# The DRAM sums of an encoder's weights: an earlier start, a wider spacing, and one issuing engine

## The chip, the cores and the metric

The kernel runs on one core of a Trainium2 chip. The metric is the device time in microseconds of one execution, the median over the runs of one kernel; fewer is better. A profile is one execution taken by the hardware profiler, with its own time.

The engines in the profile are PE (TensorE; PEld is its weight load), DVE (VectorE), ACT (ScalarE), POOL (GpSimd) and SP (SyncE, which here only issues transfers). ACT, POOL and SP each issue DMA transfers from their own instruction queue, in the order of that queue.

## What is computed

Two layers of an encoder on 256 positions of 2048 channels, in float32. Each layer has a mixer and a gated feed-forward part, with a norm ahead of each and a residual sum behind it. Cut to what matters here:

```python
for layer in range(2):
    h = rms_norm(x, norm_mix[layer])
    if layer % 2 == 0:
        ...                                  # pooling and grouped-query attention, one output projection
    else:
        mixed = mlstm_mixer(h, ...)          # matrix memory in 8 heads, gates, one output projection
    x = x + mixed
    x = x + conv_ffn(rms_norm(x, norm_ffn[layer]), w_up[layer], conv_w[layer], conv_b[layer], w_down[layer])

def conv_ffn(x, w_up, conv_w, conv_b, w_down):
    u = x @ w_up                             # 2048 -> 2 x 5632
    u = conv of width 3 over the positions of u, plus conv_b
    gate, val = jnp.split(u, 2, axis=-1)
    return (jax.nn.silu(gate) * val) @ w_down   # 5632 -> 2048
```

## The kernel before

**Weights.** All weights stream through SBUF in pieces of 128 x 1024 float32 (512 KB). `Stream.load` (line 107) issues one transfer on SP's queue, up to five pieces ahead. `Stream.split` makes a high part on ACT (line 127) and a low part, the rest, on DVE (line 128), up to two pieces ahead; these are the tiles `hl`. Every product is three matmuls (high by high, high by low, low by high), all recorded at line 256. There are six `wraw` buffers for loaded pieces and four `wsplit` buffers for split ones.

**Feed-forward layers.** The 44 pairs of up tiles are done in chunks of 4, 8, 8, 8, 8 and 8 (`FCH`). An up tile (`up`) takes four pieces and 64 matmuls, then the convolution and the gate. Between the up tiles of a chunk stand the down products of the chunk before. For some halves of the output columns these are done by a scheme that needs seven products of blocks in place of eight (`unit`, matmuls into `pp`); it needs sums of weight blocks. `_halves` says for which: half 1 in every chunk but the last, half 0 as well in the chunks 2 to 4 of layer 0 and 1 to 4 of layer 1. `unit` of half 1 runs in the first four slots of the next chunk, that of half 0 in the last four.

**Sums of weight blocks.** For half 1 they are made on the fly: `Stream.prepare` loads a piece on SP (line 112, tile `sum`, three buffers) and adds another to it by an accumulating transfer on GpSimd's queue (line 113); the further sums of that pair are made on DVE in `split` (lines 123 and 124, a `Chain`). For half 0 they are made ahead of time in DRAM by `premix`: 12 in layer 0 and 16 in layer 1, one for each pair of rows of blocks. Each takes five transfers: two copies into the scratch tile `m` (here on ACT's queue), one accumulate of a third block, and two accumulates of half a piece from `m` into `m`, all three on GpSimd's queue. `Stream.load` then reads `m` as it reads any weight (`w<-m`).

**What sets the order.** PE's instructions stand in program order. The other engines' are put in order by a scheduler when the program is built, with waits put in where data asks for them. A `Weave` holds a clock of its own: every part of a product ticks it by an estimate of its matmuls' time, and generators that were added with a delay get on when it has passed. `premix(layer, gap, late)` adds one generator a sum with `aside`: the first eight start `gap` apart and the others `late` apart, in units of that clock (about a microsecond); the steps of one lie 0.2, 1.2, 1.2 and 1.2 gaps apart. `paced` makes each of these transfers wait for the matmul that was issued last at that place of the program. The end of the last step hands the tile to `Stream.load`.

**Norms.** `Norm.finish` takes the inverse square root with a `pow` on GpSimd (line 263) between two steps of DVE. For norms 0 and 2 it sends the result through DRAM and back by two transfers on GpSimd's queue (`rr` line 340, `R` line 342). `scaled` in the mLSTM layer reads `R` (line 821).

Of the kernel before, what the change touches and what calls it, by code (L numbers as in the profile page):

```python
# [32 lines left out]
FCH = [4, 8, 8, 8, 8, 8]  # L33
# [174 lines left out]
def trunk(ctx: ExitStack, tc: tile.TileContext, gx, xT, xn, call, catt, cml, weights, mixes, out):  # L208
    nc = tc.nc
    v, a, g, pe = nc.vector, nc.scalar, nc.gpsimd, nc.tensor  # L210
# [241 lines left out]
    def paced(ins):  # L452

        tc.add_manual_dep(ins.ins, last_mm[0].ins.name, now, reason="paced")

    def premix(layer, gap, late):

        def one(i, s0, s1, r, made):
            m = scratch.tile([P, 2, CH * P], F32, tag=f"m{layer}{i}", name=f"m{layer}_{i}")
            h = CH * P // 2  # L460
            steps = [(nc.scalar, m[:, 0], s0, {}, 0.2), (nc.scalar, m[:, 1], r, {}, 1.2),
                     (g, m[:, 0], s1, add, 1.2), (g, m[:, 1, :h], m[:, 0, :h], add, 1.2),
                     (g, m[:, 1, h:], m[:, 1, :h], add, 0.0)]
            for eng, to, src, kw, wait in steps:
                paced(eng.dma_start(to, src, **kw))
                if wait:
                    yield wait * gap
            for j in range(2):
                made[j].ap = m[:, j]

        for i, e in enumerate(mixes[layer]):
            wv.aside(one(i, *e), min(i + 1, 8) * gap + max(i - 7, 0) * late)
# [275 lines left out]
    def mlstm_layer(norm, nxt):  # L748
        with ExitStack() as es:
# [171 lines left out]

            hns, done = {}, set()
            wv.add(norm.finish(), 6.0)
            premix(1, 28.0, 28.0)
            for hp in range(MH // 2):
                vf = t1p.tile([P, 2, 512], F32, tag="vf", name=f"mvf{hp}")
                for c, n in ((0, MD + 32), (MD, MD)) if hp == 0 else ((0, 512),):
# [26 lines left out]
    def ffn_layer(layer, norm, nxt):  # L954
        with ExitStack() as es:
# [16 lines left out]
            def up(c, f, gt, i):  # L972
                ps = stat_group(xx, list(range(KT)), f"up{layer}_{f}")
                wv.until(lambda: norm.R is not None)
                u = gather(tp, ps, f"up{layer}_{f}")
                v.tensor_mul(u, u, bc(norm.R, 2))  # L976
                y = tp.tile([P, 2, S], F32, tag="y", name=f"y{layer}_{f}")
                z = t1p.tile([P, 2, 2, S], F32, tag="z", name=f"z{layer}_{f}")
                for j in range(2):
                    tl = f + j * FT  # L980
                    a.activation(z[:, 0, j, :], u[:, j, :], AF.Copy, scale=cw(tl, 0))  # L981
                    a.activation(z[:, 1, j, :], u[:, j, :], AF.Copy, scale=cw(tl, 2))
                    a.activation(y[:, j, :], u[:, j, :], AF.Identity, scale=cw(tl, 1), bias=cw(tl, 3))  # L983
                v.tensor_add(y[:, :, 1:S], y[:, :, 1:S], z[:, 0, :, 0 : S - 1])  # L984
                v.tensor_add(y[:, :, 0 : S - 1], y[:, :, 0 : S - 1], z[:, 1, :, 1:S])
                if i % 2 == 0:
                    quads[c, i // 2] = tp.tile([P, 4, P], F32, tag="silu", bufs=3, name=f"s{layer}_{f}")
                s_ = quads[c, i // 2][:, i % 2 * 2 : i % 2 * 2 + 2].rearrange("p a b -> p (a b)")
                a.activation(s_, y[:, 0, :], AF.Silu)
                v.tensor_mul(s_, s_, y[:, 1, :])  # L990
                a.copy(gt[:, i, 0, :], s_)
                v.tensor_sub(gt[:, i, 1, :], s_, gt[:, i, 0, :].bitcast(F32))

            def combine(c, j):

                g4 = quads.pop((c, j))
                sf = sm1.tile([P, 512], F32, tag="sq", name=f"sf{layer}_{c}_{j}").rearrange("p (a b) -> p a b", a=4)
                v.tensor_sub(sf[:, 0:2], g4[:, 0::3], g4[:, 1:2].to_broadcast([P, 2, P]))
                v.tensor_add(sf[:, 2], sf[:, 1], g4[:, 0])
                v.tensor_sub(sf[:, 3], sf[:, 2], g4[:, 2])  # L1000
                s3 = kp.tile([P, 2, 3, P], F32R, tag=f"s3{j}", name=f"s3{layer}_{c}_{j}")
                s1 = st.sums.tile([P, 2, P], F32R, tag=f"s1{j}", name=f"s1{layer}_{c}_{j}")
                for d, e in ((s3, sf[:, 0:3]), (s1, sf[:, 3])):
                    a.copy(d[:, 0], e)
                    v.tensor_sub(d[:, 1], e, d[:, 0].bitcast(F32))
                combos[c, j] = s3, s1
# [104 lines left out]
            def down(c, b):  # L1111
                gt, last = gts[c], c == len(FCH) - 1
                kts = list(range(FCH[c]))
                if last and nxt is None and b == NB - 1:
                    down_end(gt, b, kts)
                    return
                ps = mmp.tile([P, 2, 512], F32, tag="mm", name=f"dn{layer}_{c}_{b}")
                mov_part(ps, lambda k: gt[:, k], kts, True, True)
                if last:
                    wv.until(lambda: ("total", 1) in pss)  # L1120
                residual(ps, b)
                if last and nxt is None:
                    nc.sync.dma_start(out[:, :, b * 512 : b * 512 + 512], x[:, :, b * 512 : b * 512 + 512])
                elif last:
                    nxt.add(b)

            def down_two(c):

                gt, n = gts[c], FCH[c]
                pss2 = [mmp.tile([P, 2, 512], F32, tag="mm", name=f"dn{layer}_{c}_{b}") for b in range(2)]  # L1130
                for kts in (range(n - 2), range(n - 2, n)):
                    for ps in pss2:
                        mov_part(ps, lambda k: gt[:, k], list(kts), kts[0] == 0, kts[-1] == n - 1)
                wv.until(lambda: 0 not in seen or ("total", 0) in pss)
                for b, ps in enumerate(pss2):
                    residual(ps, b)
                    if nxt is None:
                        nc.sync.dma_start(out[:, :, b * 512 : b * 512 + 512], x[:, :, b * 512 : b * 512 + 512])
                    else:
                        nxt.add(b)  # L1140
# [3 lines left out]
            for kind, c, i, *j in _ffn_plan(layer):  # L1144
                if kind == "up":
                    if i == 0:
                        gts.append(actp.tile([P, 8, 2, S], F32R, tag=f"B{c % 2}", name=f"g{layer}_{c}"))
                    up(c, f, gts[c], i)
                    f += 1
                elif kind == "down":  # L1150
                    down(c, i)
                elif kind == "two":
                    down_two(c)
                elif kind == "mix":
                    combine(c, i)
                else:
                    unit(kind, c, i, *j)
# [3 lines left out]
    attention_layer(norms[0], norms[1])  # L1161
    norms.append(Norm(2))
    ffn_layer(0, norms[1], norms[2])
    norms.append(Norm(3))
    mlstm_layer(norms[2], norms[3])
    ffn_layer(1, norms[3], None)


# [55 lines left out]
def _ffn_plan(layer):  # L1224

    seq = []  # L1230
    for c, n in enumerate(FCH):
        pairs = FCH[c - 1] // 2 if c else 0
        halves = _halves(layer, c - 1)

        if halves == (0, 1):
            slots = [[(kind, c - 1, h, js)] for h in (1, 0) for kind in "AB" for js in ((0, 1), (2, 3))]
        else:
            slots = [[(kind, c - 1, 1, (j,))] for kind in "AB" for j in range(pairs)]
            for b in range(2 if pairs else 0):
                slots[(b + 1) * pairs // 2 - 1].append(("down", c - 1, b))  # L1240

        busy = {j: k for k, slot in enumerate(slots) for u in slot if u[0] == "A" for j in u[3]}
        for i in range(n):
            seq.append(("up", c, i))
            seq += slots[i] if i < len(slots) else []
            if c < len(FCH) - 1:
                seq += [("mix", c, j) for j in range(n // 2) if i == max(2 * j + 1, busy.get(j, 0))]
    return seq + [("two", len(FCH) - 1, 0)] + [("down", len(FCH) - 1, b) for b in range(2, NB)]
# [156 lines left out]
```

## Time and profile before

| | |
|---|---|
| median of 3 runs | 2174.39 us (2172.65 to 2174.52) |
| profiled execution | 2172.38 us |
| its span, from the first to the last instruction | 2170.4 us |
| granted TensorE clock | 1.00 |
| HBM read and written over the span | 539.50 and 60.86 MB, 277 GB/s |
| stages by the span | attention layer to 260, feed-forward layer 0 to 972, mLSTM layer to 1453, feed-forward layer 1 to the end |

A busy row gives time, share of the span and number of instructions. In a row of a group, the part after the bar is the busy time and the mean of one, and after the next bar the engine's idle time just before them and what ended most of it. A name with a small q behind the engine (ACTq, POOLq, SPq) is the queue's part: it issues a transfer and the engine itself stays idle. GpSimd's own issues stand as POOL and count as busy. An arrow after an idle time points to what ended the wait. A row of transfers gives the queue that issued them, their number, the size of one and the median time from issue to landing.

### The profile page before, as it was taken

To read this page: it belongs to the slowest core of one execution; us is meant where nothing else is said; L and a number is where in the kernel's file an instruction comes from. 1 tells how busy PE (TensorE), PEld (TensorE's weight loads), DVE (VectorE), ACT (ScalarE), POOL (GpSimd) and SP (SyncE) were. 2 spreads that over 40 slices of the span, in tenths; PEclk is the share of its full clock that TensorE was granted. 3 is DMA by queue.
4 is the path that set the end of the run, shared out by engine and by line. 5 is a ranking of instruction groups with operands and counts; after the bars stand their busy time and mean duration, and the time that the engine had idled before them with its cause. 6 is when DMAs were issued, how large, how long until landed. Compare 5 with 4: busy or idle time off the path is not lost.

```text
span 2170.4 us, 31559 instructions
## 1 busy us (share of the span) xinstructions
PE 2160.9 (100%) x11424; PEld 1845.4 (85%) x11424; DVE 1729.7 (80%) x2428; ACT 1406.7 (65%) x2200; POOL 128.7 (6%) x160
## 2 busy tenths in 40 slices
PE   9999999999999999999999999999999999999999
PEld 7888888888888888889888888888888888888887
DVE  7686678887988888976777676667888898988896
ACT  7665576766677767666554554457676777776763
POOL 0011010000000000000000010110000000000000
PEclk9999999999999999999999999999999999999999
DMA  9668988787988877757688888998978787887774
GB/s 326 220 204 255 287 247 263 231 268 243 293 272 278 281 247 234 253 193 226 203 250 248 252 243 243 276 274 249 270 214 283 253 272 248 264 266 242 233 252 163
DMA packets 157790, 543.72 MB, mean 251 GB/s; under 512 B 17498, under 2 KB 19842, under 8 KB 157634
## 3 DMA queue, kind: packets, MB, share of 16 engines
q1 hardware_dynamic: 129056, 460.10, 61.1%
q0 software_dynamic: 17440, 48.51, 13.5%
q10 hardware_dynamic: 11138, 33.11, 4.6%
q8 instruction: 89, 1.46, 0.3%
q14 instruction: 67, 0.55, 0.1%
HBM read 539.50 MB, written 60.86 MB: 277 GB/s over the span
## 4 chain that ended last, share of the span: by engine, by line
PE 92%; DVE 4%; DMA 3%; issue 1%; ACT 1%; DVEq 0%; ACTq 0%; POOLq 0%
PE up L256 40%; PE pp L256 11%; PE op L256 8%; PE dn L256 6%; PE mv L256 4%; PE mq L256 4%; PE mk L256 4%; PE mo L256 4%; PE qproj L256 3%; DVE hl L128 2%; DMA w<-in_dn 1%; PE kproj L256 1%; PE vproj L256 1%; DMA sum<-in_dn 1%; PE pool L256 1%
## 5 line engine op out<-in xcount | busy, mean ns | idle before, releaser
L128 DVE TENSOR_TENSOR hl<-w,hl 128x1024 fp32r<-128x1024 f32 (+2 forms) x836 | 1002.8, 1211 | 223.3 <-ACT hl L127 220.6
L127 ACT CAST hl<-w 128x1024 fp32r<-128x1024 f32 (+2 forms) x835 | 857.2, 1043 | 450.5 <-PE up L256 134.3
L256 PE MATMUL up<-xx,hl 128*128 128x512 f32 (+1 forms) x5632 | 996.6, 337 | 3.2 <-DVE hl L128 3.0
L256 PEld LDWEIGHTS up<-xx,hl 128*128 128x128 f32 x5632 | 865.9, 188 | 137.9 <-DVE hl L128 7.9
L256 PE MATMUL pp<-hl,s 128*128 128x512 f32 x768 | 193.2, 393 | 0.4 <-DVE hl L128 0.4
L256 PEld LDWEIGHTS pp<-hl,s 128*128 128x128 f32 x768 | 141.3, 188 | 30.2 <-DVE hl L128 1.6
L256 PE MATMUL pp<-hl,g 128*128 128x512 f32 x576 | 147.9, 391 | 0.0
L419 ACT COPY tb_up<-up 128x512 f32<-128x512 f32 x88 | 51.6, 586 | 113.0 <-PE up L256 112.8
L256 PEld LDWEIGHTS pp<-hl,g 128*128 128x128 f32 x576 | 105.4, 188 | 20.7
L256 PE MATMUL dn<-hl,g 128*128 128x512 f32 x528 | 122.7, 390 | 0.0
L256 PEld LDWEIGHTS dn<-hl,g 128*128 128x128 f32 x528 | 98.7, 188 | 20.3
L983 ACT ACTIVATE y<-tb_up,cst 128x256 f32<-128x256 f32 x176 | 103.6, 589 | 0.0
L984 DVE TENSOR_TENSOR y<-y,z 128x510 f32<-128x510 f32 x88 | 60.5, 688 | 50.2 <-ACT y L983 50.2
L981 ACT ACTIVATE z<-tb_up,cst 128x256 f32<-128x256 f32 x176 | 88.4, 502 | 7.9 <-DVE tb_up L976 6.4
L256 PE MATMUL mk<-xx,hl 128*128 128x512 f32 (+1 forms) x512 | 92.1, 337 | 0.0
L256 PE MATMUL mq<-xx,hl 128*128 128x512 f32 (+1 forms) x512 | 92.1, 337 | 0.0
L256 PE MATMUL mv<-hl,xx 128*128 128x512 f32 (+2 forms) x480 | 91.7, 350 | 0.0
L256 PE MATMUL op<-hl,cat 128*128 128x512 f32 x384 | 91.6, 393 | 0.0
L420 DVE TENSOR_TENSOR tb_up<-up,tb_up 128x512 f32<-128x512 f32 x88 | 60.6, 688 | 38.4 <-ACT tb_up L419 38.4
L256 PE MATMUL mo<-hl,xx 128*128 128x512 f32 x384 | 90.5, 391 | 0.0
L256 PE MATMUL op<-hl,mcat 128*128 128x512 f32 x384 | 89.5, 392 | 0.0
L256 PEld LDWEIGHTS mq<-xx,hl 128*128 128x128 f32 x512 | 79.2, 188 | 11.6
(232 smaller groups left out, 2097.0 us busy)
## 6 DMA issues: line engine op xcount, KB each, us to landing
w<-in_up SPq DMA_DIRECT2D x352, 512.0 KB, 4.8
w<-in_dn SPq DMA_DIRECT2D x176, 512.0 KB, 4.5
w<-in_m_in SPq DMA_DIRECT2D x124, 512.0 KB, 5.3
m<-in_dn ACTq DMA_DIRECT2D x56, 512.0 KB, 6.0
w<-m SPq DMA_DIRECT2D x56, 512.0 KB, 4.8
w<-in_a_in SPq DMA_DIRECT2D x46, 512.0 KB, 4.8
sum<-in_dn SPq DMA_DIRECT2D x36, 512.0 KB, 4.9
sum<-in_dn POOLq DMA_DIRECT2D x36, 512.0 KB, 8.9
```

Of the source, the lines that this page charges most:

```text
L127: (self.nc.vector.tensor_copy if i + c == 0 else self.nc.scalar.copy)(hl[:, 0, c : c + n], w[:, c : c + n])
L128: self.nc.vector.tensor_sub(hl[:, 1, c : c + n], w[:, c : c + n], hl[:, 0, c : c + n].bitcast(F32))
L256: last_mm[0] = pe.matmul(out_, lhsT, rhs, start=start, stop=stop, skip_group_check=True)
L419: a.copy(tb, ps[:, :, 1, :])
L420: v.tensor_add(tb, ps[:, :, 0, :], tb)
L981: a.activation(z[:, 0, j, :], u[:, j, :], AF.Copy, scale=cw(tl, 0))
L983: a.activation(y[:, j, :], u[:, j, :], AF.Identity, scale=cw(tl, 1), bias=cw(tl, 3))
L984: v.tensor_add(y[:, :, 1:S], y[:, :, 1:S], z[:, 0, :, 0 : S - 1])
```

## The change

All five transfers of each sum are issued by GpSimd, in both layers. `premix` for layer 1 is called in feed-forward layer 0, in its last chunk after the up tile i = 4, and no longer at the start of the mLSTM layer; its gaps are 46 units and no longer 28. Those of layer 0 stay at 26 and 90.

```diff
         def one(i, s0, s1, r, made):
             m = scratch.tile([P, 2, CH * P], F32, tag=f"m{layer}{i}", name=f"m{layer}_{i}")
             h = CH * P // 2
-            steps = [(nc.scalar, m[:, 0], s0, {}, 0.2), (nc.scalar, m[:, 1], r, {}, 1.2),
+            steps = [(g, m[:, 0], s0, {}, 0.2), (g, m[:, 1], r, {}, 1.2),
                      (g, m[:, 0], s1, add, 1.2), (g, m[:, 1, :h], m[:, 0, :h], add, 1.2),
                      (g, m[:, 1, h:], m[:, 1, :h], add, 0.0)]
...
             wv.add(norm.finish(), 6.0)
-            premix(1, 28.0, 28.0)
             for hp in range(MH // 2):
...
                     up(c, f, gts[c], i)
                     f += 1
+                    if layer == 0 and c == len(FCH) - 1 and i == 4:
+                        premix(1, 46.0, 46.0)
                 elif kind == "down":
```

## Prediction

> **What bounds the kernel now.** I read the page first (busy time, chain that ended last, costliest groups), then a table of busy time by stage, then the rows of the moved transfers.
>
> ```profile
> PE 2160.9 (100%) x11424; PEld 1845.4 (85%) x11424; DVE 1729.7 (80%) x2428; ACT 1406.7 (65%) x2200; POOL 128.7 (6%) x160
> ...
> PE 92%; DVE 4%; DMA 3%; issue 1%; ACT 1%; DVEq 0%; ACTq 0%; POOLq 0%
> ...
> L256 PE MATMUL up<-xx,hl 128*128 128x512 f32 (+1 forms) x5632 | 996.6, 337 | 3.2 <-DVE hl L128 3.0
> ```
>
> TensorE (PE) is busy for 2160.9 of 2170.4 us; the other rows hang on it. What a change of transfers can win is bounded by PE's idle time, so I ask where that lies. The columns of the next view are the stretch, its length, busy us (and instructions) of PE, PEld, DVE, ACT and POOL, the granted clock, the DMA share and GB/s.
>
> ```profile
> 0.00:57.00 57.00, 55.78 (x239) 44.98 (x240) 42.32 (x79) 41.41 (x91) 5.44 (x13) 1.00 0.93 316
> 57.00:460.00 403.00, 402.07 (x2139) 344.00 (x2138) 299.44 (x450) 260.36 (x461) 41.14 (x47) 1.00 0.81 246
> 460.00:590.00 130.00, 129.59 (x693) 110.70 (x692) 110.35 (x145) 87.95 (x135) 8.46 (x10) 1.00 0.83 262
> 590.00:718.00 128.00, 127.42 (x678) 108.23 (x677) 111.79 (x148) 93.89 (x143) 6.74 (x8) 1.00 0.87 281
> 718.00:972.00 254.00, 253.30 (x1317) 214.88 (x1316) 223.03 (x290) 178.58 (x273) 2.85 (x4) 1.00 0.73 243
> 972.00:1608.00 636.00, 636.00 (x3448) 548.90 (x3448) 456.69 (x693) 356.81 (x520) 52.49 (x65) 1.00 0.81 246
> 1608.00:1735.00 127.00, 126.95 (x679) 108.56 (x678) 108.45 (x143) 92.63 (x145) 3.82 (x5) 1.00 0.81 262
> 1735.00:1860.00 125.00, 123.94 (x659) 105.35 (x658) 112.97 (x150) 89.73 (x137) 3.41 (x4) 1.00 0.81 261
> 1860.00:1986.00 126.00, 125.39 (x668) 107.08 (x667) 113.50 (x150) 91.83 (x139) 3.44 (x4) 1.00 0.81 261
> 1986.00:2170.00 184.00, 180.50 (x919) 152.71 (x918) 151.14 (x188) 113.44 (x163) 0.85 (x1) 1.00 0.65 217
> ```
>
> From 972 to 1608 (mLSTM layer and the first part of the last feed-forward layer) PE has no idle time, and the DRAM sums of layer 1 are made in just that stretch. From 57 to 972, where those of layer 0 are made, PE idles 0.93 + 0.41 + 0.58 + 0.70 = 2.62 us. The rest is start, end and 0.05 + 1.06 + 0.61 us in 1608 to 1986, where one moved transfer lies. So even if every stall near a moved transfer went, the gain would be 2.6 us, 0.12%. Both sides of 0.2% (4.3 us, about what a measurement of this kernel can tell from no change) are judged by what the change adds.
>
> **The issue of the first two transfers, from ScalarE's queue to GpSimd's.** The columns are the queue, the operation, tiles, count, ns (least, median, most) and first and last start.
>
> ```profile
> L465 ACTq DMA_DIRECT2D m<-in_dn x56: 497/497/595, 57.5 to 1498.9; - x56
> L465 POOL DMA_DIRECT2D m<-in_dn x28: 812/818/1192, 107.4 to 1534.7; - x28
> ...
> POOL m L465 <- PE up L256: 458.0, 30, 33.3
> ...
> m<-in_dn ACTq DMA_DIRECT2D x56, 512.0 KB, 6.0
> ...
> m<-in_dn POOLq DMA_DIRECT2D x28, 512.0 KB, 9.0
> m<-m POOLq DMA_DIRECT2D x56, 256.0 KB, 7.2
> ```
>
> Removed from ScalarE: 56 x 0.497 = 27.8 us of issue, and 56 waits for a matmul (`paced`). ScalarE is 65% busy and not where PE waits: worth nothing up to the 2.6 us above; I take 0.3, since 972 to 1608 has no PE idle to give back. Added to GpSimd: 56 x 0.818 = 45.8 us on an engine 6% busy. That is hidden by GpSimd's idle time; but each issue also holds GpSimd's queue until its matmul has run, and behind it may stand three things: the `pow` of an inverse square root, for which VectorE waits in order; the two transfers that spread the norm (`rr`, `R`); and the accumulate of an on-the-fly `sum`. GpSimd already does this 84 times (28 + 56), with 458 us of such waits in the matmuls named `up` alone, and PE is not hurt.
>
> The bandwidth is not changed: the bytes are the same. The landing time of a plain copy on GpSimd's queue is in no row. Its ends are the ACT row (6.0 us) and the accumulating row (9.0 us); I take 6.0, as it does no adding. Nothing waits for it before the next step, 55.2 units of the schedule later.
>
> [...]
>
> **The norm behind the new start.** The sums of layer 1 now start before the mLSTM layer's norm. Its steps are on GpSimd:
>
> ```profile
> 978.64 0.71 POOL L263 TENSOR_TENSOR ry_n<-rv_n,mhalf 128x2 f32<-128x2 f32 x1 [96.66 <-DVE rv_n L261]
> ...
> 981.62 0.80 POOL L340 DMA_DIRECT2D rr<-re_n  x1 [2.26 <-DVE nrcol L940]
> ...
> 991.14 0.57 POOL L342 DMA_DIRECT2D R<-rr  x1 [8.72 <-DMA rr<-re_n]
> ...
> 1016.42 0.68 DVE L821 SCALAR_TENSOR_TENSOR tb_q<-tb_q,R 128x512 f32<-128x512 f32 x1
> ```
>
> `R` is issued at 991.1 and, taking the 7.2 us of a small GpSimd transfer, is there at 998; it is first used at 1016.4. The 18 us in between cover one paced issue ahead of each of the three steps. Cost 0; without that cover some 2 us.
>
> **The new place and spacing of layer 1's sums.** Before; in the third row the use of the last four sums, then the up tile in which the new call lies, cut off by the view's window, and a whole up tile of 64 matmuls:
>
> ```profile
> L465 ACTq DMA_DIRECT2D m<-in_dn x32: 497/498/558, 1008.1 to 1498.9; - x32
> L465 POOL DMA_DIRECT2D m<-m x32: 802/814/1194, 1096.6 to 1607.6; - x32
> ...
> L107 SPq DMA_DIRECT2D w<-m x8: 319/323/327, 2052.1 to 2077.1; - x8
> ...
> 865.49 7.70 PE L256 MATMUL up<-xx,hl 128*128 128x512 f32 x43
> ...
> 1754.71 11.30 PE L256 MATMUL up<-xx,hl 128*128 128x512 f32 x64
> ```
>
> From the first copy of sum 0 to the second of sum 15 are 15 x 28 + 5.6 = 425.6 units of the schedule in 490.8 us: 1.153 us a unit. The up tile i = 4 of the last chunk starts at 865.5 and runs 11.3 us, so `premix` is called at 876.8. Its first copy comes 46 units later, at 930; the second copy of sum 15 at 930 + (15 x 46 + 9.2) x 1.153 = 1736; and the last step (165.6 units on, at the (1607.6 - 1498.9) / 100.8 = 1.08 us a unit of that tail) at 1914. Its tile is loaded at about 2052, so 138 us remain: no load comes to wait for a sum.
>
> What moves is the company. In 972 to 1608 there are fewer transfers, which wins nothing. But past 1608, where one was, some 22 now lie: about 12 in 1608 to 1735, 7 in 1735 to 1860, 3 after (80 steps placed at 46 i + 0, 9.2, 64.4, 119.6 and 174.8 units). Each chunk there has a burst of some 40 us in which the on-the-fly sums are refilled, with little slack in the fourth:
>
> ```profile
> 1746.54 0.33 SPq L112 DMA_DIRECT2D sum<-in_dn  x1
> ...
> 1751.69 0.85 POOL L113 DMA_DIRECT2D sum<-in_dn  x1 [106.43 <-DVE sf L998]
> ...
> 1760.31 0.69 DVE L123 TENSOR_TENSOR w<-w,sum 128x512 f32<-128x512 f32 x1 [1.97 <-DMA w<-in_dn]
> ...
> 1761.99 1.22 DVE L128 TENSOR_TENSOR hl<-w,hl 128x1024 fp32r<-128x1024 f32 x1
> ```
>
> The sum is loaded at 1746.5, accumulated from 1751.7, and at 1760.3 VectorE, idle for 1.97 us, gets on; the name is of `w`, but the sum's accumulate lands about then too. Behind it on VectorE stands the split that the up tile begun at 1754.7 needs for its last quarter, from 1754.7 + 11.3 x 3/4 = 1763.2 on; it ends at 1763.2. A later landing would be a PE stall of nearly its own length. How much later it gets with sums in the making I read from the DMA views of a chunk that has them (460 to 590, the first two rows) and one that has not (1608 to 1735):
>
> ```profile
> sum<-in_dn POOLq DMA_DIRECT2D x6, 512.0 KB, 9.7
> sum<-in_dn SPq DMA_DIRECT2D x5, 512.0 KB, 5.6
> ...
> sum<-in_dn SPq DMA_DIRECT2D x4, 512.0 KB, 4.4
> sum<-in_dn POOLq DMA_DIRECT2D x4, 512.0 KB, 8.4
> ```
>
> (9.7 - 8.4) + (5.6 - 4.4) = 2.5 us for one such chain. So the ends are 0 and, for three bursts, 7.5 us. Against the upper end speaks PE's idle time itself: 0.41 and 0.58 us in the chunks of layer 0 with sums beside them (460 to 718), 0.05, 1.06 and 0.61 us in those of layer 1 without. I take 0.7 us a burst for three bursts, 2.1 us, nearer to the lower end because that row is PE's own.
>
> **The sum.** -0.3 + 0 + 0 + 2.1 = +1.8 us on the profiled execution's 2172.4 us (span 2170.4), that is 2174.2. The median of the runs, 2174.4, stands 2.0 us above that execution; against it the forecast is 2176.2 us.
>
> **The rivals.**
>
> First, slower: the fourth sum's chain becomes the wait that ends last in the bursts after 1608. It decides as soon as that accumulate lands over 0.4 us later, the start of one matmul pair. For it: the 2.5 us and a split that is done just when it is used. Against it: the same chain beside sums in layer 0 left PE idle for half a us. At 2.5 us in two to three bursts it gives +5 to +7.5: 2180.7 us in the middle. Chance 0.25.
>
> [...] Copies are two of five transfers and an accumulate is issued four times a chunk, so few meet: chance 0.08. [...]
>
> Third, faster: ScalarE's waits and issues did cost the 2.62 us of 57 to 972, and the bursts are unhurt: 2171.8 us. Chance 0.06; a gain over 0.2% would need more idle time than there is beside the moved transfers, so only 0.03 for that.
>
> Fourth, the change does not do what it says, a sum being made later than its load: excluded by the 138 us.
>
> **How the numbers follow.** The forecast, within 0.2% either way, has the other 0.61. Same: 0.61 plus half of the third, 0.64. Slower by over 0.2%: 0.25 + 0.08 = 0.33. Faster: 0.03. The range runs from 2171.8 (the third rival) to 2183.5, past the first rival's end (2181.9) and short of the second's.
>
> **What would show it.** ACTq loses all 56 issues, POOL issues 84 of the `m<-in_dn` instead of 28, at about 0.82 us each. First transfer of layer 1 near 930, last near 1914. PE idle in 972 to 1608 stays under 0.5 us; in 1608 to 1986 it goes from 1.72 to about 3.8 us. [...] I am wrong if PE idles in the attention stage or near 980, behind GpSimd's `pow` or `R`, or if the time falls by over 4.3 us.

## The result and the profile after

| | before | after |
|---|---|---|
| median of 6 runs each | 2174.45 us (2172.65 to 2177.16) | 2183.59 us (2178.87 to 2185.00) |
| profiled execution, span | 2172.38, 2170.4 us | 2185.00, 2183.2 us |

The change makes the kernel slower: the ratio is 1.0036, with a 95% interval of 1.0023 to 1.0049, some 9.1 us by the medians. The forecast was +1.8 us; the time lies 0.09 us above the range given. The profiled execution of after is the longest of its six.

The page of after, in the lines that answer to those of before: busy time, the chain that ended last, the two groups that changed, and two rows of transfers.

```profile
PE 2165.4 (99%) x11424; PEld 1847.7 (85%) x11424; DVE 1729.8 (79%) x2428; ACT 1407.4 (64%) x2200; POOL 161.2 (7%) x216
...
PE 88%; DMA 5%; DVE 5%; issue 1%; ACT 1%; DVEq 0%; ACTq 0%; POOLq 0%
...
L256 PE MATMUL up<-xx,hl 128*128 128x512 f32 (+1 forms) x5632 | 999.7, 337 | 11.9 <-DVE hl L128 9.9
...
L465 POOL DMA_DIRECT2D m<-in_dn x84 | 55.8, 664 | 788.5 <-PE up L256 268.1
...
m<-in_dn POOLq DMA_DIRECT2D x84, 512.0 KB, 7.1
```

PE waits 11.9 us ahead of the `up` matmuls where it waited 3.2, and 9.9 of these for VectorE's split (line 128). On the chain, transfers and VectorE have taken 10% where they had 7%. The second view is the same table of stretches as in the prediction, of after.

```profile
57.00:460.00 403.00, 402.64 (x2140) 344.26 (x2139) 299.09 (x450) 260.87 (x460) 52.94 (x65) 1.00 0.82 246
460.00:590.00 130.00, 129.38 (x689) 109.95 (x688) 110.01 (x145) 88.28 (x136) 10.63 (x14) 1.00 0.82 259
590.00:718.00 128.00, 126.82 (x671) 107.37 (x671) 111.60 (x147) 91.62 (x140) 7.84 (x10) 1.00 0.88 280
718.00:972.00 254.00, 251.98 (x1310) 213.51 (x1309) 221.38 (x287) 178.15 (x272) 3.94 (x6) 1.00 0.76 247
972.00:1608.00 636.00, 636.00 (x3446) 548.97 (x3445) 455.44 (x693) 358.19 (x522) 54.00 (x75) 1.00 0.78 232
1608.00:1735.00 127.00, 123.77 (x654) 105.78 (x654) 107.81 (x143) 90.23 (x141) 12.09 (x16) 0.99 0.91 286
1735.00:1860.00 125.00, 121.47 (x642) 102.51 (x642) 107.83 (x144) 85.23 (x128) 9.22 (x11) 1.00 0.87 274
1860.00:1986.00 126.00, 124.41 (x663) 106.04 (x662) 112.09 (x147) 90.72 (x139) 4.29 (x5) 1.00 0.81 262
```

From 1608 to 1986 PE idles 3.23 + 3.53 + 1.59 = 8.35 us, where it idled 1.72: 6.63 us more. The DMA share of the first of these chunks has gone from 0.81 to 0.91. Ahead of 972 it idles 4.18 us, where it idled 2.62. From 972 to 1608 there is still none.

A landmark splits the loss of the profiled execution. It is the last norm's step of line 265 on VectorE, at the end of the mLSTM layer, in the timelines of before and then of after:

```profile
1457.37 0.16 DVE L265 TENSOR_TENSOR re_n<-ry_n 128x2 f32<-128x2 f32 x1 [0.90 <-POOL ry_n L263]
```

```profile
1460.80 0.16 DVE L265 TENSOR_TENSOR re_n<-ry_n 128x2 f32<-128x2 f32 x1 [0.90 <-POOL ry_n L263]
```

3.4 us are lost by there and 12.8 - 3.4 = 9.4 us behind it. The 9.4 us are of the size of the medians' 9.1. The 3.4 us, with the 1.56 us of idle time ahead of 972 in them, are in this one execution. Experiment 7 below, which differs from after only in the sums 9 to 15 (from about 1407 us on), passes this step at 1457.3 us, as before does.

**The burst at 1625.** The timeline of after: start, us, engine, line, operation; in brackets the idle time before, and what ended it.

```profile
1623.56 0.88 POOL L113 DMA_DIRECT2D sum<-in_dn  x1 [8.71 <-DVE hl L128]
...
1624.77 0.87 POOL L465 DMA_DIRECT2D m<-in_dn  x1 [0.33 <-PE pp L256]
...
1627.08 0.33 SPq L107 DMA_DIRECT2D w<-in_dn  x1
...
1629.13 6.21 PE L256 MATMUL up<-xx,hl 128*128 128x512 f32 x34
...
1632.55 1.04 ACT L127 CAST hl<-sum 128x1024 fp32r<-128x1024 f32 x1
...
1635.90 0.69 DVE L123 TENSOR_TENSOR w<-w,sum 128x512 f32<-128x512 f32 x1 [3.76 <-DMA w<-in_dn]
...
1637.31 2.35 DVE L128 TENSOR_TENSOR hl<-w,hl 128x1024 fp32r<-128x1024 f32 x2
...
1638.58 2.68 PE L256 MATMUL up<-xx,hl 128*128 128x256 f32 x8 [3.23 <-DVE hl L128]
```

The chain's add (line 123) takes a loaded piece and a sum. The sum was there by 1632.55, when ScalarE split it. The piece, issued at 1627.08, was not, and VectorE stood 3.76 us for it. Behind that add, in VectorE's order, stands the split that the running up tile needs for its second half. It gets done late, and PE stands 3.23 us. What made the piece late is seen in its time to landing, in the DMA view of the moment of its issue. First its row of after, then that of the same piece before, issued at 1623.4:

```profile
w<-in_dn SPq DMA_DIRECT2D x1, 512.0 KB, 8.7
```

```profile
w<-in_dn SPq DMA_DIRECT2D x1, 512.0 KB, 6.1
```

The piece took 2.6 us longer, beside an accumulate of a moved sum (`m<-in_dn`, 1624.77) that was not there before. In before, VectorE waited 1.15 us for it and PE not at all (timeline of before):

```profile
1629.58 0.69 DVE L123 TENSOR_TENSOR w<-w,sum 128x512 f32<-128x512 f32 x1 [1.15 <-DMA w<-in_dn]
```

The three chunks are not alike. In the trace of after 12, 7 and 1 transfers of moved sums are issued in them. The one of the third comes at 1899.7, behind that chunk's pause (1.59 us, up to 1896.8). There too a chain's piece landed late, 6.1 us after its issue at 1888.8 where before has 4.2, but with no moved transfer issued since 1849.1. So 5.65 of the 6.63 us lie in the two chunks that have the moved transfers, and 0.98 us are not theirs.

**The clock behind the pause.** The table of stretches once more, after, around 1638.58; the third number from the end is the granted clock:

```profile
1635.00:1638.00 3.00, 0.34 (x2) 0.00 (x0) 2.10 (x4) 0.52 (x2) 0.33 (x1) 1.00 1.00 299
...
1638.60:1640.00 1.40, 1.40 (x6) 1.21 (x7) 1.40 (x2) 0.31 (x1) 0.00 (x0) 0.61 1.04 218
1640.00:1642.00 2.00, 2.00 (x8) 1.71 (x8) 2.00 (x4) 0.00 (x0) 0.00 (x0) 0.50 1.09 321
1642.00:1643.00 1.00, 1.00 (x6) 0.86 (x5) 0.87 (x1) 0.23 (x1) 0.00 (x0) 0.84 0.98 373
```

Right after the pause the granted clock was 0.50, from 1638.90 to 1642.31: 1.40 x 0.39 + 2.00 x 0.50 + 1.00 x 0.16 = 1.7 us of PE's work were lost, and PE counts as busy meanwhile. So of the 9.4 us 6.63 are idle time, 1.7 the clock, and 1.1 are not placed.

### The profile page after: what moved, and what is told of

The parts are those of the page before. It is cut to its first block, busy times and chain, and to the rows that moved or that the text cites. A ratio compares the mean times of both kernels' runs of the same rounds, so it can differ in the third digit from the quotient of the medians.

```text
span 2183.2 us, 31568 instructions
## 1 busy us (share of the span) xinstructions
PE 2165.4 (99%) x11424; PEld 1847.7 (85%) x11424; DVE 1729.8 (79%) x2428; ACT 1407.4 (64%) x2200; POOL 161.2 (7%) x216
## 4 chain that ended last, share of the span: by engine, by line
PE 88%; DMA 5%; DVE 5%; issue 1%; ACT 1%; DVEq 0%; ACTq 0%; POOLq 0%
PE up L256 38%; PE pp L256 11%; PE op L256 8%; PE dn L256 5%; PE mv L256 4%; PE mq L256 4%; PE mk L256 4%; PE mo L256 4%; PE qproj L256 3%; DVE hl L128 2%; DMA w<-in_dn 2%; DMA w<-in_up 2%; DMA sum<-in_dn 1%; PE kproj L256 1%; PE vproj L256 1%
## 5 line engine op out<-in xcount | busy, mean ns | idle before, releaser
L256 PE MATMUL up<-xx,hl 128*128 128x512 f32 (+1 forms) x5632 | 999.7, 337 | 11.9 <-DVE hl L128 9.9
L465 POOL DMA_DIRECT2D m<-in_dn x84 | 55.8, 664 | 788.5 <-PE up L256 268.1
```

What stands on the lines that cost most here:

```text
L256: last_mm[0] = pe.matmul(out_, lhsT, rhs, start=start, stop=stop, skip_group_check=True)
```

## The experiments

The theory: the transfers that the wider spacing puts into the chunks past 1608 make a chain's piece land late, and VectorE's order turns that into a pause of PE. The rivals: the one queue for all transfers (GpSimd's) costs the time, or the early place does. Each experiment is an edit of before or of after, timed beside before on the same chip. "Idle" is PE's idle time in the three chunks from 1608 to 1986, 1.72 us before and 8.35 after.

**1. The engine alone.** Before, with GpSimd issuing all five transfers.

```diff
-            steps = [(nc.scalar, m[:, 0], s0, {}, 0.2), (nc.scalar, m[:, 1], r, {}, 1.2),
+            steps = [(g, m[:, 0], s0, {}, 0.2), (g, m[:, 1], r, {}, 1.2),
```

> The engine alone is changed: GpSimd issues all five transfers, layer 1's sums keep their old place and spacing. Theory A (the loss is the company of the moved transfers past 1608 us, where the fourth on-the-fly sum of a burst lands late and VectorE, waiting for it in order at line 123, holds up a split that PE needs): the part past 1608 goes, PE idle from 1608 to 1986 is back under 2.5 us, and the time is 0 to 4 us over the kernel before. Rival B (the copies on GpSimd's queue are what costs, by standing in front of accumulates or holding the queue): most of the loss stays, 6 to 10 us over.

Measured: 2174.49 us against 2175.64, ratio 0.9992 (0.9984 to 1.0001); idle 0.05 + 1.21 + 0.71 = 1.97 us. The issuing engine costs nothing, and the rival of GpSimd's queue falls.

**2. The place and spacing alone.** After, with ScalarE issuing the two copies again (the edit of experiment 1 undone).

> The new place and spacing alone: ScalarE issues the first two transfers as before. Theory A: the accumulates in the bursts past 1608 us are as late as in the changed kernel, 5 to 10 us over the kernel before. Rival B: 0 to 3 us over.

Measured: 2183.53 us against 2175.64, ratio 1.0036 (1.0023 to 1.0048): the whole loss. Idle 2.39 + 2.79 + 0.86 = 6.04 us, and the granted clock was 0.99 over each of the first two chunks (0.50 from 1638.0 to 1638.6). The burst is hit in the same way, with a piece that took 9.2 us to land (timeline of this kernel):

```profile
1633.93 0.69 DVE L123 TENSOR_TENSOR w<-w,sum 128x512 f32<-128x512 f32 x1 [3.60 <-DMA w<-in_dn]
...
1635.81 6.93 PE L256 MATMUL up<-xx,hl 128*128 128x256 f32 x30 [2.38 <-DVE hl L128]
```

**3. The early place without the spacing.** After, with the gaps of before.

```diff
-                        premix(1, 46.0, 46.0)
+                        premix(1, 28.0, 28.0)
```

> The changed kernel with the spacing of layer 1's sums put back to 28 units; the new place and GpSimd stay. The last transfer then comes near 1540 us, ahead of the three bursts. Theory A: as with the engine alone, 0 to 4 us over the kernel before, and PE idle from 1608 to 1986 under 2.5 us. Rival B: 6 to 10 us over. If the early place itself cost something, near the mLSTM layer's norm, PE idle would show between 972 and 1100.

Measured: 2174.75 us against 2175.64, ratio 0.9992 (0.9983 to 1.0001); idle 0.05 + 0.92 + 0.59 us. The sums are done by 1509, and the loss is gone. So the early start is free too, and the spacing carries all of it.

**4. The chain's add kept in the program's order.** After, with the add of line 123 pinned to its place in the program on VectorE, so that it no longer goes ahead of earlier work.

```diff
-            self.nc.vector.tensor_add(w[:, :half], w[:, :half], self.sum[:, :half])
+            self.keep(self.nc.vector.tensor_add(w[:, :half], w[:, :half], self.sum[:, :half]))
```

> The changed kernel, and the first DVE addition of a chain (line 123), which reads the on-the-fly sum, is kept behind what stands before it in the program, so that no split of an earlier weight waits behind it on VectorE. The transfers are untouched. Theory A in its narrow form (a late sum turns into a PE stall only because VectorE's queue is in order): at least half of the loss goes, the time is at most 4 us over the kernel before. Rival C (weights and sums are late altogether, for lack of transfer rate in the bursts): 6 to 10 us over, with PE idle before the products of the sum itself.

Measured: 2195.43 us, ratio 1.0091 (1.0077 to 1.0105), a miss. The groups of this kernel:

```profile
L256 PE MATMUL up<-xx,hl 128*128 128x512 f32 (+1 forms) x5632 | 998.4, 337 | 0.8 <-DVE hl L128 0.5
...
L256 PE MATMUL pp<-hl,s 128*128 128x512 f32 x768 | 198.8, 396 | 17.0 <-ACT hl L127 11.0 <-DVE hl L128 5.8
```

The idle time ahead of `up` falls from 11.9 to 0.8 us, as it should if the add's place makes it. But now the add comes too late for its own piece, and PE pauses 17.0 us ahead of `pp`, in every burst, whether transfers of sums lie beside it or not (at 2029, where there are none, by 1.68 us). The pin exchanges one wait for another and does not settle the question.

**5 and 6. The add just ahead of its sum's own split,** in after (5) and in before (6): a fixed early place.

```diff
+    def chain(self, i, w):
+        if isinstance(self.srcs[i], Chain) and i not in self.chained:
...
+            self.keep(self.nc.vector.tensor_add(w[:, :half], w[:, :half], self.sum[:, :half]))
...
+        self.chain(i, w)
+        i + 1 in self.w and self.chain(i + 1, self.w[i + 1][0])
```

> The changed kernel with the DVE additions of a chain put at one fixed place: just ahead of the split of the on-the-fly sum that they belong to, behind all splits of earlier weights. That split needs the same sum, so no new wait is made, and no split of an earlier weight waits for the sum any more. The transfers are untouched. Theory A in its narrow form (the late sum costs because VectorE waits for it ahead of a split that PE needs first): the idle time before the matmuls named up past 1608 us (11.9 us in all in the changed kernel) falls under 4 us, and the time is 0 to 4 us over the kernel before. Rival C (the weights themselves come too late beside the transfers): 6 to 10 us over, with PE idle before other splits.

> The kernel before with the same fixed place of the chain's additions. Theory A: its small stalls ahead of the matmuls named up (3.2 us in all, 0.5 to 0.8 us a burst) go, 0 to 3 us under the kernel before. If the fixed place has a price of its own, as pinning the additions to the place in the program had, it shows here as 3 us or more over.

Measured: 2307.47 and 2308.33 us, ratios 1.0606 (1.0592 to 1.0621) and 1.0609 (1.0594 to 1.0623). Both are far from what was expected. The order itself costs some 133 us whatever the transfers do: PE's idle time ahead of `pp<-hl,s` is 101.6 us in experiment 5. They say nothing of the theory, and only that an order fixed by hand on VectorE is dear here.

**7. The bytes.** After, with the transfers of the late sums of layer 1 (9 to 15) reduced in bytes, not in number. The kernel leaves these sums out and loads an unsummed block in place of each.

```diff
-                paced(eng.dma_start(to, src, **kw))
+                k = to.shape[-1] // (8 if layer and i >= 9 else 1)
+                paced(eng.dma_start(to[:, :k], src[:, :k], **kw))
...
-                made[j].ap = m[:, j]
+                made[j].ap = (s0, r)[j] if layer and i >= 9 else m[:, j]
```

> The changed kernel, in which the transfers of layer 1's sums from number 9 on move an eighth of their columns; these sums are left out of the computation and their unsummed blocks are used instead. Number, places, waits and issuing engine of the transfers are unchanged. Theory A, as a matter of bytes (the accumulate of an on-the-fly sum is late since it shares the transfer engines): the loss goes, 0 to 3 us over the kernel before. Rival D (the order of issue on GpSimd's queue, its waits for matmuls, or the fixed time of a transfer): 5 to 10 us over.

Measured: 2174.52 us against 2175.01, ratio 0.9999 (0.9990 to 1.0008); idle 0.05 + 1.22 + 0.57 us. The transfers stand at the same places with the same waits, on the same queue, and cost nothing once they are small. The chain's piece lands as it should, as the DMA view of this kernel at 1623.1 shows:

```profile
w<-in_dn SPq DMA_DIRECT2D x1, 512.0 KB, 5.0
```

So it is the bytes of the late transfers that cost, not their number, their waits or their order on GpSimd's queue.

One more thing differs, which no edit asked for. In the first burst of after and of experiments 2 and 8 the scheduler has put some small operations of VectorE in another order than in before and in experiments 1, 3 and 7. In after, for example, a step `y<-y,z` of the convolution runs at 1630.31, ahead of the late add at 1635.90; in before it runs at 1630.19, behind that add (1629.58). What this alone costs was not measured. It does not explain the landing: the piece took 8.7 us in after, 9.2 in experiment 2 and 7.8 in experiment 9, where VectorE's order is a third one, against 6.1 in before and 5.0 here. And the late add stands between the same two splits in before, in after and here.

**8. A spacing in between.** After, with gaps of 37, so that only the first of the three bursts has sums beside it (the last transfer is issued at 1703.2).

> The changed kernel with a spacing of 37 units: some five transfers come past 1608 us, the last near 1705, so that only the first of the three bursts has company. Theory A: PE idle from 1608 to 1735 is 1.5 to 4 us as in the changed kernel, from 1735 on as in the kernel before; the time is 2 to 5 us over the kernel before. If the loss grew with the spacing itself and not with the bursts that are hit, it would be half of the changed kernel's at every place.

Measured: 2181.37 us against 2175.01, ratio 1.0027 (1.0016 to 1.0039), +6.4 us, above what was expected. Idle 4.08 + 1.85 + 0.05 us. The first burst is hit by the theory's mechanism, but one chain earlier: the piece issued at 1603.3, beside an accumulate of a moved sum (1602.3), took 7.7 us to land (3.5 before), and VectorE stood 3.39 us for it. PE's pauses behind that are 0.87, 0.59 and 2.62 us, the last of them with a piece that landed in 6.2 us, about as before. The third burst is not hit. The second has a pause of 1.85 us in place of 0.69 before, though the last transfer of a sum lies 40 us ahead of it and VectorE's order is that of before; its piece took 5.8 us to land (4.6 before), and why is open. That pause is nearly that of after at the same place, but the clock behind it differs. First experiment 8, then after, the same 62 matmuls:

```profile
1747.50 12.53 PE L256 MATMUL up<-xx,hl 128*128 128x256 f32 x62 [1.85 <-DVE hl L128]
```

```profile
1747.48 10.96 PE L256 MATMUL up<-xx,hl 128*128 128x256 f32 x62 [1.68 <-DVE hl L128]
```

Behind 1.85 us the granted clock was 0.50 (table of stretches, 1748.6 to 1751.8), behind 1.68 us it stayed at 1.00 (1747.5 to 1750.7 of after), and the 62 matmuls took 12.53 us in the one and 10.96 in the other, 1.57 us more. In the first chunk too the granted clock of experiment 8 was 0.99, where the 46 matmuls behind the pause of 2.62 us took 9.72 us. If that cost as much, some 3.3 us of its loss are clock, an estimate.

**9 and 10. The order where it matters, and no more.** After (9) and before (10), with one edge of order on VectorE: the chain's first add may not stand ahead of the split (line 128) of the piece four earlier. It adds no wait between engines.

```diff
-            self.nc.vector.tensor_add(w[:, :half], w[:, :half], self.sum[:, :half])
+            self.behind(self.nc.vector.tensor_add(w[:, :half], w[:, :half], self.sum[:, :half]), self.low[i - 4])
...
-            self.nc.vector.tensor_sub(hl[:, 1, c : c + n], w[:, c : c + n], hl[:, 0, c : c + n].bitcast(F32))
+            self.low[i] = self.nc.vector.tensor_sub(hl[:, 1, c : c + n], w[:, c : c + n], hl[:, 0, c : c + n].bitcast(F32))
```

> The changed kernel, with one thing more: the first DVE addition of a chain may not stand on VectorE's queue ahead of the split of the weight four pieces earlier (an order edge without a wait). It then stands two splits later than it did, still well ahead of its own use. The transfers are untouched. Theory A in its narrow form: the pauses ahead of the matmuls named up past 1608 us go, and the time is -2 to 3 us against the kernel before, without the price that the two stricter orders had. Rival C (weights and sums too late altogether): 6 to 10 us over.

> The kernel before with the same order edge. Theory A: its small pauses ahead of the matmuls named up go, 1 to 4 us under the kernel before. If the edge has a price of its own it shows here.

Measured, against 2174.24 us: 2169.58 with the change, ratio 0.9978 (0.9968 to 0.9988); 2167.50 without it, ratio 0.9967 (0.9955 to 0.9979). The DMA view of experiment 9 at the issue of the chain's piece (1623.4), the add that takes it, and then its table of stretches:

```profile
w<-in_dn SPq DMA_DIRECT2D x1, 512.0 KB, 7.8
```

```profile
1631.82 0.69 DVE L123 TENSOR_TENSOR w<-w,sum 128x512 f32<-128x512 f32 x1
```

```profile
1608.00:1735.00 127.00, 127.00 (x680) 108.89 (x680) 110.59 (x146) 93.21 (x144) 12.94 (x17) 1.00 0.95 303
1735.00:1860.00 125.00, 124.15 (x663) 106.00 (x662) 112.37 (x149) 89.86 (x137) 8.41 (x10) 1.00 0.89 279
1860.00:1986.00 126.00, 126.00 (x673) 107.96 (x672) 114.74 (x152) 91.13 (x138) 4.29 (x5) 1.00 0.83 267
```

The transfers are where after has them, the DMA share is even higher (0.95), and the piece still takes 7.8 us. Yet PE idles 0.85 us in the three chunks where it idled 8.35. The lateness has stayed, and the pause has gone: VectorE does other work until the piece is there, and it was its order that made the one into the other. Before, too, gains from the edge. The chain that ended last and the group of `up` in experiment 10:

```profile
PE 97%; DVE 2%; DMA 1%; issue 0%; ACT 0%; DVEq 0%; ACTq 0%
...
L256 PE MATMUL up<-xx,hl 128*128 128x512 f32 (+1 forms) x5632 | 994.2, 337 | 0.5 <-DVE hl L128 0.5
```

The idle time ahead of `up` falls from 3.2 to 0.5 us and the busy time of these matmuls from 996.6 to 994.2, together 5.1 of the 5.5 us by which the span is shorter. Experiment 10 is the fastest kernel here. Even with the edge the change looks some 2.1 us the slower of the two by the medians, though the two intervals overlap.

## Why the prediction was wrong in size

- **The bound.** PE bound, and nothing to win at the moved transfers: right. PE's idle time from 972 to 1608 is 0 in both.
- **The issue (-0.3) and the plain copy on GpSimd (0).** Right to cost nothing (experiment 1: within 0.1% or so). The durations were off: the 48 `m<-in_dn` of layer 1 have a median of 0.55 us on GpSimd, not 0.82, since the plain copies' issues were shorter than the accumulating ones' (in after 0.53 us at 1614.3, 0.87 at 1624.8). That changes no term.
- **The norm (0).** Right: no idle time near 980 to 1016. The 7.2 us taken for `R` is the row of pieces of 256 KB; the `R` issued at 991.1 took 7.1 before.
- **The place.** First transfer of layer 1 at 929.8 (about 930 predicted), last at 1899.7 (1914). In the three chunks past 1608 are 12, 7 and 1 of them (12, 7 and 3). No load waited for a sum.
- **The bursts (+2.1): the step that failed.** The 0.7 us a burst was set by PE's idle time in the chunks of layer 0 that have sums beside them (0.41 and 0.58 us), as the row that "is PE's own". Measured: 6.63 us in place of 2.1, of which 5.65 lie in two bursts. That is 2.8 us for each burst that has company, above the upper end of 2.5, which was read from landing times. The row of layer 0 did not carry over, though its chunks have 8 and 6 such transfers in them and these 12 and 7; why is not known. The prediction's own reading of the chain at 1760, a VectorE wait of 1.97 us with a split behind it that ends just when it is used, was the nearer row, and it said that lateness beyond 0.4 us would be PE's.
- **A term that was missing.** The granted clock of 0.50 behind a pause, 1.7 us in the profiled execution of after. Its clock over the span was 0.999; that of experiment 2 was 0.998.
- **The first rival** (chance 0.25; +5 to +7.5 us) is what happened, by its mechanism: over 6 us of idle, ahead of line 128. Two points of it were off. It looked to the sum's accumulate, but what is late is the loaded piece of the chain (8.7 for 6.1 us), with the sum there 3.3 us earlier. And its price left out the clock; with it, 6.6 + 1.7 comes near the 9.1.
- **The second rival** (chance 0.08), copies ahead of accumulates on GpSimd's queue, falls with experiments 1 to 3. No run shows in which order the transfers of one queue finish, or what a copy ahead would cost an accumulate; the rival's end, which the range stops short of, is a term that no run shows. What the runs show is the time: in experiment 1 GpSimd issues all five transfers and nothing is lost (ratio 0.9992), in experiment 2 ScalarE issues the copies and all is lost (1.0036).

Left open: why pieces landed 1.9 and 1.2 us later with no moved transfer beside them (third burst of after, second of experiment 8), what the other order of VectorE's small operations adds, the 1.1 us not placed, and what made the granted clock fall to 0.50.

## What to carry to other kernels

Look at what stands behind an instruction whose data may come late. Here it was work that the bounding engine needed first, and the lateness became a pause of nearly the same length (3.76 us on VectorE, 3.23 on PE); one edge of order gained more than any spacing that was tried. When transfers are moved, ask in which stretches their bytes come to lie and how much slack the loads have there; here the issuing queue and the start did not matter (ratio 0.9992 in experiments 1 and 3).

## What the runs showed of the hardware

In three of these kernels a short pause of PE cost more than itself. In after, behind a pause of 3.23 us, the granted clock was 0.50 for 3.41 us (1638.90 to 1642.31), which cost 1.7 us. In experiment 2, behind 2.38 us, it was 0.63 over 1635.0 to 1638.0, 0.50 to 1638.6 and 0.78 to 1640.0: 3.00 x 0.37 + 0.60 x 0.50 + 1.40 x 0.22 = 1.7 us again. In experiment 8, behind 1.85 us, it was 0.50 from 1748.6 to 1751.8, and the 62 matmuls there took 1.57 us longer than in after. Over the chunks with the pauses of 1.93 us in experiment 2 (1735 to 1860) and 2.62 us in experiment 8 (1608 to 1735) it was 0.99.

Behind 1.68 us (after, 1747.5) it was 1.00. Before and experiments 1, 3, 7, 9 and 10 had 1.000 over the span of their profiled executions; the longest pause of before from 57 us on was 0.86 us.

Experiment 4 has two pauses close together, 1.74 us up to 559.26 and 0.76 us up to 560.52. The 64 `up` matmuls behind them took 12.20 us, where the 64 ahead of them took 11.30, and the granted clock over 460 to 590 was 0.99. How long a pause has to be, and whether its length alone decides, was not shown.
